# Sinks apart from the table exponential, wide norm statistics between large products, and late windowed output adds on GpSimd, in a hybrid attention and ConvFFN layer

## The chip, the cores and the metric

The kernel runs on one core of a Trainium2 chip. Four compute engines work side by side, each on its own queue of instructions in program order: TensorE (PE in the profile; its weight loads are PEld), VectorE (DVE), ScalarE (ACT) and GpSimd (POOL). SyncE (SP) issues most of the DMAs. Engines meet only at semaphores, so an engine that waits holds back all that is queued behind the waiting instruction. Matmul results lie in PSUM, everything else in SBUF.

The metric is device time in microseconds (us) of one execution, as the median over several. The profile comes from one further execution, whose time is given beside it.

## The reference

One layer over 1024 latent tokens of width 1024, with 256 context tokens that serve as keys and values only. The layer's input is modulated by a conditioning vector. It then goes through two attention branches in parallel, a gated merge, a first norm, a gated ConvFFN and a second norm. Cut to what the change touches:

```python
def _sink_softmax(scores, sink):
    sink = sink.astype(jnp.float32)[:, :, None, None]
    m = jnp.maximum(jnp.max(scores, axis=-1, keepdims=True), sink)
    e = jnp.exp(scores - m)
    return e / (jnp.sum(e, axis=-1, keepdims=True) + jnp.exp(sink - m))

def _layer_norm(x, g, b):
    mu = jnp.mean(xf, axis=-1, keepdims=True)
    var = jnp.mean(jnp.square(xf - mu), axis=-1, keepdims=True)
    return ((xf - mu) * lax.rsqrt(var + LN_EPS) * g + b).astype(x.dtype)

h = x * (1.0 + scale1) + shift1
# branch A: 8 heads on 2 key heads, keys within 128 tokens and the context, sinks
o_a = _windowed_attention(q_a, k_a, v_a, k_a_c, v_a_c, sink)
# branch B: 8 heads on 2 key heads, all keys and the context
o_b = _global_attention(q_b, concat([k_b, k_b_c]), concat([v_b, v_b_c]))
y = (g_a * (o_a @ w_branch_a) + g_b * (o_b @ w_branch_b)) @ w_out
x = _layer_norm(ALPHA * x + gate1 * y, ln1_g, ln1_b)
y = _conv_ffn(x * (1.0 + scale2) + shift2, w_up, conv_w, conv_b, w_down)
x = _layer_norm(ALPHA * x + gate2 * y, ln2_g, ln2_b)
```

## The kernel before

**Arithmetic.** Every large float32 product is made of three fp32r matmuls: an operand is split into a high and a low part, and `mm3` (L89 to L92) adds high x high, high x low and low x high in PSUM. The split itself is `split` (L77 to L87): a copy gives the high part (L82 on ScalarE, L84 on GpSimd), a subtraction the low part (L87 on VectorE or GpSimd). A big matmul has 512 columns.

**Stages, in program order.** First the modulation and the input projections, with the gates in `sgd` on DRAM. Then attention, with the output projection of each branch (`b`) filled in between. Then the merge and `w_out` (`y`) with the first norm, the ConvFFN with its products, and the second norm at the end.

**Attention.** 32 units `Unit(br, i, g)` run one after another: branch 0 (windowed, units 0_0_0 to 0_7_1) and then branch 1 (global, 1_0_0 on). `i` is one of 8 blocks of 128 tokens and `g` one of two key heads, with four query heads each. Where the branch is plain, a unit is written by i and g alone, (6,1) for 0_6_1; so are the tile names in the listings of the change (`up_6_0`). The profile prints tile names without any of these numbers. For each head `lat` makes the scores on TensorE (`s`, L494 and L495), VectorE scales them and takes their maximum (L545, tile `p`), and ScalarE takes the exponential with its sum (L547). In branch 0 each row of probabilities gets one more column, the sink of the head, which GpSimd writes two at a time (L542, from `sinkb`). `norm` (L562) inverts the sums. `rows` puts them as rows into `rb` by way of DRAM.

The steps of unit u's scores are laid between the value steps of the unit before. A value step (`tr_step`) transposes a block of 128 keys for four heads on TensorE (L605, into PSUM tile `ptr`, three buffers) and splits it: ScalarE writes the high part `pth` (L614), VectorE the low part `ptl` (L615). In branch 0, block 3 of the units with `i` from 1 to 6 (in branch 1 two blocks of each unit but the last) goes another way and is called `pooled`: ScalarE copies it into one of two `side` tiles in SBUF (L611), and GpSimd makes both parts (L84 and L87). After a lag of some steps `av_step` multiplies both parts with the values (L626, L627) into the one PSUM tile `av`. After a unit's last block `out_step` copies `av` to a `side` tile (L638 on ScalarE), GpSimd moves its upper half to `up` (L639), two adds join the halves into `ot` (L642; VectorE in branch 0, GpSimd in branch 1 but for the last unit), GpSimd multiplies by `rb` (L645) and splits into the operands `O` (L84, L87). `side` has two tiles in turn, `up` and `ot` one buffer each. The next units' queries are transposed on TensorE (`qtr`), copied by ScalarE (L487, tile `q`), and scaled or split on GpSimd (`qs`).

Between the gates' last sigmoid and attention's first exponential, L871 makes exp(-2^100) = 0 in `zero`, with the load of ScalarE's table of exponentials in front of it. L872 adds this zero to `sinkb` on GpSimd.

**The norms.** `ln_add` sums each finished slice of z and its squares into `zs` and `zq`. `ln_steps` returns the steps of one slice's norm: `stats` (sums over the features by TensorE, one matmul of one column for each 128 tokens and each of `zs` and `zq`, L1186 and L1187, tile `st`, then some small operations), `diags`, `cast` (broadcast of the rows) and eight `apply` steps. Each step carries a distance. A list `pend` holds the steps and a counter `clock`; after each `mm3` of a large product, `tick` adds HALF / 0.8 = 640 for its 512 columns, and a step is issued as soon as the counter reaches its distance, which is then taken off. The order on TensorE is thus fixed when the program is built. The first norm has slices a0 (512 tokens) and smaller ones, the second b0 (512 tokens) and two of 256.

The lines that the change edits stand in `tr_step` (L608), `out_step` (L640), behind `zero` (L872) and in `ln_steps` (L1179 to L1186, L1218):

```python
pooled = n in POOL_LO[self.br] and not last and (self.br or 0 < self.i < NT - 1)
oe = nc.gpsimd if self.br and not last else nc.vector
nc.gpsimd.tensor_tensor(out=sinkb[:, 0:4], in0=sinkb[:, 0:4], in1=zero, op=ALU.add)
for t in range(n):
    ts = slice(s.start + t * P, s.start + (t + 1) * P)
    nc.tensor.matmul(st[:, t:t + 1], zs[:, ts], onec, start=True, stop=True)
    nc.tensor.matmul(st[:, n + t:n + t + 1], zq[:, ts], onec, start=True, stop=True)
```

Of the kernel before, what the change touches and what calls it, by code (L numbers as in the profile page):

```python
# [10 lines left out]
ALU = mybir.AluOpType  # L11
AX = mybir.AxisListType

P = 128
# [4 lines left out]
NT = 8  # L19
# [8 lines left out]
HALF = 512  # L28
FBIG = 3.0e38
POOL_LO = (3,), (2, 6)  # L30
# [39 lines left out]
def layer_kernel(  # L70
# [6 lines left out]
    nc = tc.nc  # L77
# [27 lines left out]
    sinkb = ctile([P, 8], F32, "sinkb")  # L105
# [7 lines left out]
    onec = ctile([P, 1], F32, "onec")  # L113
# [171 lines left out]
    for k in range(KT):  # L285
# [10 lines left out]
        for a in (0, 4):  # L296
            ts = [slice(t * P, (t + 1) * P) for t in range(a, a + 4)]
# [166 lines left out]
    class Unit:  # L464
# [131 lines left out]
        def value_steps(self):  # L596
            nm, kt = self.id, self.kt
            vh = self.br * 2 + self.g
            last = self.id == f"1_{NT - 1}_1"
            parts = {}  # L600

            def tr_step(n):
                tr = pt_tile(f"ptr{nm}_{n}")
                for h in range(4):
                    nc.tensor.transpose(tr[:, h * P:(h + 1) * P], self.pslice(h, n), ident)  # L605
                hi = att.tile([P, 512], R32, tag="pth", name=f"pth{nm}_{n}", bufs=4)
                lo = att.tile([P, 512], R32, tag="ptl", name=f"ptl{nm}_{n}", bufs=4)
                pooled = n in POOL_LO[self.br] and not last and (self.br or 0 < self.i < NT - 1)  # L608
                if pooled:
                    rw = side_tile()  # L610
                    nc.scalar.copy(rw, tr)  # L611
                    split(rw, hi, lo, nc.gpsimd, nc.gpsimd)
                else:
                    nc.scalar.copy(hi, tr)  # L614
                    nc.vector.tensor_tensor(out=lo, in0=tr, in1=hi.bitcast(F32), op=ALU.subtract)  # L615
                parts[n] = hi, lo
                return pooled

            def av_step(n):
                first = self.left == len(kt)  # L620
                self.left -= 1
                if first:
                    self.av = ps2.tile([P, 512], F32, tag="av", name=f"av{nm}")
                hi, lo = parts.pop(n)
                v = VT[kt[n] // 2][:, kt[n] % 2, vh]
                nc.tensor.matmul(self.av, v, hi, start=first, stop=False)  # L626
                nc.tensor.matmul(self.av, v, lo, start=False, stop=self.left == 0)  # L627

            def out_step():
                av = self.av  # L630
                up = att.tile([HD, 512], F32, tag="up", name=f"up{nm}", bufs=1)
                ot = att.tile([P, 2, P], F32, tag="ot", name=f"ot{nm}", bufs=1)
                if last:
                    low = av
                    nc.scalar.copy(up, av[HD:P])
                else:
                    low = side_tile()
                    nc.scalar.copy(low, av)  # L638
                    nc.gpsimd.tensor_scalar(out=up, in0=low[HD:P], scalar1=1.0, scalar2=0.0, op0=ALU.mult, op1=ALU.add)  # L639
                oe = nc.gpsimd if self.br and not last else nc.vector  # L640
                for h in range(2):
                    oe.tensor_tensor(out=ot[h * HD:(h + 1) * HD],  # L642
                                     in0=low[0:HD].rearrange("p (a b q) -> p a b q", b=2, q=P)[:, :, h],
                                     in1=up.rearrange("p (a b q) -> p a b q", b=2, q=P)[:, :, h], op=ALU.add)
                (nc.vector if last else nc.gpsimd).tensor_tensor(out=ot, in0=ot, in1=self.rb, op=ALU.mult)  # L645
                hf = self.i // 4
                qs = slice((self.i % 4) * P, (self.i % 4 + 1) * P)
                split(ot, otile(self.br, hf, 0, self.g)[:, :, qs], otile(self.br, hf, 1, self.g)[:, :, qs],
                      *((nc.scalar, nc.vector) if last else (nc.gpsimd, nc.gpsimd)))

            def step(ns):
                pooled = [tr_step(n) for n in ns]
                for n, pl in zip(ns, pooled):
                    clk[0] += 1
                    avq.append((self, n, clk[0] + LAG[self.br] + (PLAG[self.br] if pl else 0)))
                    av_issue()

            self.left = len(kt)
            self.av_step, self.out_step = av_step, out_step
            g = 1 + self.br  # L660
            steps = [lambda n=n: step(range(n, n + g)) for n in range(0, len(kt), g)]
            steps.insert(3 if self.br else 2 if self.i else len(steps), self.rows)
            return steps
# [155 lines left out]
    for n, (gi, k) in enumerate(order):  # L819
# [8 lines left out]
        if gi == "g":  # L828
            for hf in (0, 1):
                last = gate(k, hf)  # L830
# [8 lines left out]
        nm, src, tiles = groups[gi]  # L839
# [4 lines left out]
        for t in tiles:  # L844
            if t < NT:
                s = slice(t * P, (t + 1) * P)
                a = hT[k][0][:, s], hT[k][1][:, s]
            else:
                s = slice((t - NT) * P, (t - NT + 1) * P)
# [19 lines left out]
    zero = ph1.tile([P, 4], F32, tag="zero", name="zero")  # L869
    nc.vector.tensor_scalar(out=zero, in0=last[:, 0:4], scalar1=-(2.0 ** 100), scalar2=None, op0=ALU.min)  # L870
    nc.scalar.activation(zero, zero, AF.Exp)  # L871
    nc.gpsimd.tensor_tensor(out=sinkb[:, 0:4], in0=sinkb[:, 0:4], in1=zero, op=ALU.add)  # L872
    hTp.release()
    ph1.release()
    ps1.release()
# [100 lines left out]
    for u in range(nu + 1):  # L976
# [8 lines left out]
        if u == 31:  # L985
            first = branch_steps(1, w_b, (0, 1), att, (nc.gpsimd, nc.gpsimd), (0,))
# [15 lines left out]
        while adds:  # L1002
            t, m = adds.pop(0)
# [50 lines left out]
    def sml(name, w=512):  # L1054
        return ps3.tile([P, w], F32, tag="sml", name=name, bufs=2)
# [41 lines left out]
    for f in range(2, KT):  # L1097
# [4 lines left out]
        for hs in halves:  # L1102
            n = HALF * len(hs)
# [36 lines left out]
    def ln_flush():  # L1140
        while sqs:
            sqs.pop(0)()
# [30 lines left out]
    def ln_steps(zs, zq, s, nm, emit, first, gap, gap1, gap2, each, pm=2, order=range(KT)):  # L1173
        w = s.stop - s.start
        n = w // P
        bcs = []
        sv = []

        def stats():  # L1179
            ln_flush()  # L1180
            sv.extend(tiny(f"{a}{nm}") for a in ("mv", "m2", "rs", "mr"))
            mv, m2, rs, mr = sv
            st = sml(f"st{nm}")
            for t in range(n):
                ts = slice(s.start + t * P, s.start + (t + 1) * P)
                nc.tensor.matmul(st[:, t:t + 1], zs[:, ts], onec, start=True, stop=True)  # L1186
                nc.tensor.matmul(st[:, n + t:n + t + 1], zq[:, ts], onec, start=True, stop=True)  # L1187
            nc.vector.tensor_scalar(out=mv[:, 0:2 * n], in0=st[:, 0:2 * n], scalar1=1.0 / D, scalar2=None,
                                    op0=ALU.mult)
            nc.vector.tensor_tensor(out=m2[:, 0:n], in0=mv[:, 0:n], in1=mv[:, 0:n], op=ALU.mult)  # L1190
            nc.vector.scalar_tensor_tensor(out=rs[:, 0:n], in0=mv[:, n:2 * n], scalar=LN_EPS, in1=m2[:, 0:n],
                                           op0=ALU.add, op1=ALU.subtract)
            nc.gpsimd.tensor_tensor(out=rs[:, 0:n], in0=rs[:, 0:n], in1=mhalf[:, 0:n], op=ALU.pow)
            nc.vector.tensor_tensor(out=mr[:, 0:n], in0=mv[:, 0:n], in1=rs[:, 0:n], op=ALU.mult)

        def diags():
            bcs.extend(diag(c[:, 0:n], n, f"{a}{nm}") for a, c in zip("rm", sv[2:]))

        def cast():
            both = sml(f"bc{nm}") if 2 * w <= HALF else None  # L1200
            for i, a in enumerate("rm"):
                ps = sml(f"bc{a}{nm}")[:, 0:w] if both is None else both[:, i * w:(i + 1) * w]
                nc.tensor.matmul(ps, onesf, bcs[i], start=True, stop=True)
                bcs[i] = ps
            mean = post.tile([P, HALF], F32, tag="mrs", name=f"mb{nm}", bufs=2)[:, 0:w]
            nc.scalar.copy(mean, bcs[1])
            bcs.append(mean)

        def apply(f):
            zf = zv(f, s)  # L1210
            nc.vector.tensor_tensor(out=zf, in0=zf, in1=bcs[0], op=ALU.mult)
            if (f + 1) % pm:
                nc.vector.tensor_tensor(out=zf, in0=zf, in1=bcs[1], op=ALU.subtract)
            else:
                nc.gpsimd.tensor_tensor(out=zf, in0=zf, in1=bcs[2], op=ALU.subtract)
            emit(f, s)

        return [(first, stats), (gap, diags), (gap1, cast)] + [(gap2 if n == 0 else each, lambda f=f: apply(f))  # L1218
                                                for n, f in enumerate(order)]

    zs, zq = tm("zs1"), tm("zq1")
# [121 lines left out]
    for f in (4, 6):  # L1343
        for si in (1, 2):
# [3 lines left out]
            elif f == 6:  # L1348
                (_, st), (_, dg), (_, ca), *ap = ln1(si)
                n = len(pend) - 4  # L1350
# [375 lines left out]
    s = LN2_S[-1]  # L1726
# [10 lines left out]
    st = pst(ab[2], "stl")  # L1737
# [57 lines left out]
    sv = [post.tile([P, 2 * nt], F32, tag=f"{n}l", name=f"{n}l") for n in ("mv", "m2", "rs")]  # L1795
# [142 lines left out]
```

## Time and profile before

| | |
|---|---|
| Time, median of 3 runs (lowest to highest) | 1548.82 us (1548.79 to 1549.32) |
| Profiled execution: its time, its span | 1549.4 us, 1547.5 us |
| Granted TensorE clock over the span | 0.996 |
| Windowed attention starts (first exponential) | 335.7 us |
| Passage from windowed to global attention | about 445 to 480 us |
| Statistics of slice a0 of the first norm | 833.3 to 835.5 us |
| Statistics of slice b0 of the second norm | 1475.6 to 1477.3 us |

How the rows of the profile are read. A row of the timeline has the start (us from the span's start), the duration in us, engine, line, operation, what is written and read, shape and type, how many instructions it stands for, and in brackets how long the engine had been idle before it and who ended that wait ("<-ACT p L547" is ScalarE's instruction of line 547). A row of a stretch has its bounds, its length, TensorE's busy time with the number of its instructions, the granted clock as a share of full speed, the busy share of the DMA engines and the GB/s that they moved. Matmuls are pipelined: a row's duration may be longer than the distance to the next start.

### The profile page before, as it was taken

The numbers are of one execution on the slowest core, as the hardware profiler recorded it, in microseconds if no ns is written. First come the engines' busy times: TensorE is split into PE (matmuls) and PEld (weight loads), VectorE is DVE, ScalarE is ACT, GpSimd is POOL, SyncE is SP. The second block draws the span as 40 slices with busy tenths as digits, with TensorE's granted clock in tenths as the row PEclk, the third lists the DMA queues.
The fourth block names the chain that finished last, engine by engine and source line by source line (L and its number), as shares of the span: only waits on it lengthen the run. The fifth ranks groups of instructions, "written<-read, shape, count | busy, mean of one in ns | idle before, by whom it ended". The sixth has DMA issues, their size and how long they took to land.

```text
span 1547.5 us, 22251 instructions
## 1 busy us (share of the span) xinstructions
PE 1528.1 (99%) x7804; PEld 1281.6 (83%) x7804; DVE 1173.3 (76%) x1768; ACT 786.6 (51%) x1271; POOL 751.3 (49%) x738
## 2 busy tenths in 40 slices
PE   9999999999999999999999999999999999999997
PEld 7888888888877888888888998888888888888887
DVE  6677976538888777777774788888888887657884
ACT  5322222458977676667332564444444444435552
POOL 0356522517765666666233345666677674111121
PEclk9999999999999999999999999999999999999998
DMA  9777673322234576563550322333344447996731
GB/s 372 266 240 245 204 252 88 103 75 70 64 85 116 125 167 135 137 150 81 207 177 14 107 88 94 110 112 117 109 106 112 110 109 204 356 266 209 257 103 55
DMA packets 114400, 232.09 MB, mean 150 GB/s; under 512 B 13201, under 2 KB 28049, under 8 KB 114193
## 3 DMA queue, kind: packets, MB, share of 16 engines
q1 hardware_dynamic: 99056, 201.82, 39.2%
q0 software_dynamic: 10400, 20.19, 8.7%
q10 hardware_dynamic: 4832, 8.68, 1.5%
q8 instruction: 61, 1.00, 0.3%
q14 instruction: 51, 0.41, 0.1%
HBM read 179.45 MB, written 65.86 MB: 159 GB/s over the span
## 4 chain that ended last, share of the span: by engine, by line
PE 89%; DVE 3%; issue 3%; ACT 3%; POOL 1%; DMA 1%; SPq 0%; DVEq 0%; ACTq 0%; POOLq 0%
PE ptr L605 6%; PE p L90 4%; PE p L92 4%; PE p L91 4%; PE g L91 3%; PE g L90 3%; PE g L92 3%; PE av L626 3%; PE b L90 3%; PE av L627 3%; PE b L91 3%; PE b L92 3%; PE s L495 2%; PE s L494 2%; PE c L90 2%
## 5 line engine op out<-in xcount | busy, mean ns | idle before, releaser
L547 ACT ACTIVATE p<-p,nm 128x1280 f32<-128x1280 f32 (+2 forms) x128 | 139.1, 1088 | 27.7 <-DVE p L545 27.1
L615 DVE TENSOR_TENSOR ptl<-ptr,pth 128x512 fp32r<-128x512 f32 x194 | 129.3, 685 | 29.7 <-ACT pth L614 27.6
L605 PE MATMUL ptr<-ident,p 128*128 128x128 f32 x944 | 141.0, 276 | 2.6 <-ACT p L547 1.2
L614 ACT CAST pth<-ptr 128x512 fp32r<-128x512 f32 x194 | 110.4, 586 | 44.3 <-PE ptr L605 35.6
L87 DVE TENSOR_TENSOR ld<-rd,hd 128x1024 fp32r<-128x1024 f32 x77 | 94.8, 1249 | 49.9 <-ACT hd L82 47.8
L605 PEld LDWEIGHTS ptr<-ident,p 128*128 128x128 f32 x944 | 108.7, 140 | 28.5 <-ACT q L487 5.4
L82 ACT CAST hd<-rd 128x1024 fp32r<-128x1024 f32 x77 | 79.4, 1050 | 80.3 <-PE p L92 54.0
L87 POOL TENSOR_TENSOR wlg<-wg,whg 128x512 fp32r<-128x512 f32 x32 | 46.6, 1467 | 123.3 <-ACT whg L82 123.3
L626 PE MATMUL av<-pth,VT 128*128 128x512 f32 x236 | 103.8, 440 | 1.3 <-ACT side L638 0.8
L90 PE MATMUL p<-hd 128*128 128x512 f32 x264 | 103.2, 391 | 0.0
L92 PE MATMUL p<-hd,ld 128*128 128x512 f32 x264 | 102.7, 389 | 0.0
L91 PE MATMUL p<-ld,hd 128*128 128x512 f32 x264 | 102.7, 389 | 0.0
L90 PE MATMUL g<-hh,whg 128*128 128x512 f32 x256 | 99.9, 390 | 0.0
L92 PE MATMUL g<-hh,wlg 128*128 128x512 f32 x256 | 99.7, 389 | 0.0
L91 PE MATMUL g<-hl,whg 128*128 128x512 f32 x256 | 99.6, 389 | 0.0
L627 PE MATMUL av<-ptl,VT 128*128 128x512 f32 x236 | 97.4, 413 | 1.5 <-POOL ptl L87 1.4
L545 DVE TENSOR_SCALAR_CACHE_REDUCE p<-s,cvt,nmc 128x1024 f32<-128x1024 f32 x64 | 84.2, 1317 | 10.6 <-PE s L495 10.4
L494 PE MATMUL s<-KL,q 128*128 128x512 f32 (+2 forms) x192 | 75.0, 390 | 0.6 <-DVE p L545 0.6
L495 PE MATMUL s<-KL,q 128*128 128x512 f32 (+2 forms) x192 | 72.0, 375 | 0.0
L82 ACT CAST wS<-s 128x512 fp32r<-128x512 f32 x76 | 45.3, 620 | 50.9 <-POOL s L1237 50.1
L782 ACT ACTIVATE sg<-g,bgc 128x512 f32<-128x512 f32 x32 | 21.9, 686 | 96.2 <-PE g L92 91.5
L82 ACT CAST wA<-ru 128x512 fp32r<-128x512 f32 x57 | 35.5, 623 | 63.2 <-PE d L92 34.4
(438 smaller groups left out, 4878.6 us busy)
## 6 DMA issues: line engine op xcount, KB each, us to landing
wml<-in_wmodT_dram SPq DMA_DIRECT2D x48, 512.0 KB
ru<-in_w_up_dram SPq DMA_DIRECT2D x38, 512.0 KB
rd<-td SPq DMA_DIRECT2D x55, 256.0 KB
rd<-sd SPq DMA_DIRECT2D x44, 256.0 KB
rd<-in_w_dn_dram SPq DMA_DIRECT2D x33, 256.0 KB
wm<-in_wmodT_dram SPq DMA_DIRECT2D x16, 512.0 KB
wg<-in_w_g_dram SPq DMA_DIRECT2D x32, 256.0 KB
sgd<-sg ACTq DMA_DIRECT2D x32, 256.0 KB
```

The source lines that it names most:

```text
L82: nc.scalar.copy(hi, src)
L87: lo_eng.tensor_tensor(out=lo, in0=src, in1=hi.bitcast(F32), op=ALU.subtract)
L90: nc.tensor.matmul(ps, a[0], b[0], start=start, stop=False, skip_group_check=resumed)
L91: nc.tensor.matmul(ps, a[0], b[1], start=False, stop=False, skip_group_check=resumed)
L92: nc.tensor.matmul(ps, a[1], b[0], start=False, stop=stop, skip_group_check=resumed)
L494: nc.tensor.matmul(o, self.q[0][:, hs], ks, start=True, stop=False)
L547: nc.scalar.activation(row, row, AF.Exp, bias=self.nm[:, hs], scale=-1.0, accum_out=self.sm[:, hs])
L605: nc.tensor.transpose(tr[:, h * P:(h + 1) * P], self.pslice(h, n), ident)
L614: nc.scalar.copy(hi, tr)
L615: nc.vector.tensor_tensor(out=lo, in0=tr, in1=hi.bitcast(F32), op=ALU.subtract)
L626: nc.tensor.matmul(self.av, v, hi, start=first, stop=False)
L627: nc.tensor.matmul(self.av, v, lo, start=False, stop=self.left == 0)
```

## The change

Four edits. First, the condition `pooled` for branch 0 counts units instead of blocks and ends with 0_6_0, so that unit 0_6_1 no longer splits its block 3 on GpSimd; it is then split on ScalarE and VectorE like the others. Second, the adds of `out_step` go to GpSimd for the last four units of branch 0 too (0_6_0 to 0_7_1). Third, the add of `zero` to `sinkb` is gone, while `zero` itself, its exponential and the table load stay. Fourth, in slices of 512 tokens the pairs of statistics matmuls become steps of their own, 640 apart in `tick`'s counter; the last pair stays in `stats`. Slices of 256 tokens are as before.

```diff
-                pooled = n in POOL_LO[self.br] and not last and (self.br or 0 < self.i < NT - 1)
+                pooled = n in POOL_LO[self.br] and not last and (self.br or 2 <= 2 * self.i + self.g < 2 * NT - 3)
...
-                oe = nc.gpsimd if self.br and not last else nc.vector
+                oe = nc.gpsimd if (self.br or self.i >= NT - 2) and not last else nc.vector
...
     nc.scalar.activation(zero, zero, AF.Exp)
-    nc.gpsimd.tensor_tensor(out=sinkb[:, 0:4], in0=sinkb[:, 0:4], in1=zero, op=ALU.add)
...
+        def stat_mm(t):
+            if t == 0:
+                ln_flush()
+                sv.append(sml(f"st{nm}"))
+            st = sv[0]
+            ts = slice(s.start + t * P, s.start + (t + 1) * P)
+            nc.tensor.matmul(st[:, t:t + 1], zs[:, ts], onec, start=True, stop=True)
+            nc.tensor.matmul(st[:, n + t:n + t + 1], zq[:, ts], onec, start=True, stop=True)
+
         def stats():
-            ln_flush()
+            for t in range(0 if n < 4 else n - 1, n):
+                stat_mm(t)
+            st = sv.pop()
             sv.extend(tiny(f"{a}{nm}") for a in ("mv", "m2", "rs", "mr"))
             mv, m2, rs, mr = sv
-            st = sml(f"st{nm}")
-            for t in range(n):
-                ts = slice(s.start + t * P, s.start + (t + 1) * P)
-                nc.tensor.matmul(st[:, t:t + 1], zs[:, ts], onec, start=True, stop=True)
-                nc.tensor.matmul(st[:, n + t:n + t + 1], zq[:, ts], onec, start=True, stop=True)
...
-        return [(first, stats), (gap, diags), (gap1, cast)] + [(gap2 if n == 0 else each, lambda f=f: apply(f))
+        lead = [(HALF / 0.8 if t else first, lambda t=t: stat_mm(t)) for t in range(n - 1 if n >= 4 else 0)]
+        return lead + [(HALF / 0.8 if lead else first, stats), (gap, diags), (gap1, cast)] + [(gap2 if n == 0 else each, lambda f=f: apply(f))
                                                 for n, f in enumerate(order)]
```

**GpSimd at the passage.** Before, GpSimd's queue holds there the output of unit 6_0 (`up`, `ot`, `O`) with the split of block 3 of unit 6_1 (`pth_6_1_3`, `ptl_6_1_3`) in between, and then the query split of the third global unit, 1_1_0 (`qs_1_0`):

```order
L639 TENSOR_SCALAR up_6_0_4788<-side 64x512
L84 TENSOR_SCALAR pth_6_1_3_4816<-side 128x512
L645 TENSOR_TENSOR ot_6_0_4789<-ot_6_0_4789,rb_6_0_4635 128x256
L87 TENSOR_TENSOR ptl_6_1_3_4817<-side,pth_6_1_3_4816 128x512
L84 TENSOR_SCALAR O_4287<-ot_6_0_4789 128x2x128
L87 TENSOR_TENSOR O_4288<-ot_6_0_4789,O_4287 128x2x128
L84 TENSOR_SCALAR qs_1_0_5048<-Q_0_544 128x4x64
```

And with the change, GpSimd at the same place:

```order
L639 TENSOR_SCALAR up_6_0_4787<-side 64x512
L642 TENSOR_TENSOR ot_6_0_4788<-side,up_6_0_4787 64x256 x2
L645 TENSOR_TENSOR ot_6_0_4788<-ot_6_0_4788,rb_6_0_4634 128x256
L84 TENSOR_SCALAR O_4286<-ot_6_0_4788 128x2x128
L87 TENSOR_TENSOR O_4287<-ot_6_0_4788,O_4286 128x2x128
L84 TENSOR_SCALAR qs_1_0_5046<-Q_0_544 128x4x64
```

The two splits of 6_1 are gone, and the two adds of 6_0 have come in ahead of L645.

**VectorE at the passage.** Before, VectorE has the adds of 6_0 (`ot_6_0`) between the sums of unit 7_0 (`sm_7_0`) and the low parts of 6_1 and 7_0:

```order
L562 RECIPROCAL sm_7_0_4710<-sm_7_0_4710 128x4
L642 TENSOR_TENSOR ot_6_0_4789<-side,up_6_0_4788 64x256 x2
L615 TENSOR_TENSOR ptl_6_1_4_4830<-ptr_6_1_4_4824,pth_6_1_4_4829 128x512
L615 TENSOR_TENSOR ptl_7_0_0_4843<-ptr_7_0_0_4837,pth_7_0_0_4842 128x512
L545 TENSOR_SCALAR p_7_1_0_4854,nm_7_1_4835<-s_7_1_0_4848,negsink 128x512
```

With the change VectorE has at this place:

```order
L562 RECIPROCAL sm_7_0_4709<-sm_7_0_4709 128x4
L615 TENSOR_TENSOR ptl_6_1_3_4816<-ptr_6_1_3_4810,pth_6_1_3_4815 128x512
L615 TENSOR_TENSOR ptl_6_1_4_4828<-ptr_6_1_4_4822,pth_6_1_4_4827 128x512
L615 TENSOR_TENSOR ptl_7_0_0_4841<-ptr_7_0_0_4835,pth_7_0_0_4840 128x512
L545 TENSOR_SCALAR p_7_1_0_4852,nm_7_1_4833<-s_7_1_0_4846,negsink 128x512
```

The two adds are gone, and the low part of block 3 of 6_1 has come in their place.

**TensorE at slice a0 of the first norm.** Before, the four pairs (`zs`, `zq` into `sta`) stand in a row between two groups of the `w_out` product `y`:

```order
L92 MATMUL y_512_512_9112<-mh_8702,lwo_8710 128x512
L1186 MATMUL sta_9136<-onec,zs_8811 128x1
L1187 MATMUL sta_9136<-onec,zq_8812 128x1
L1186 MATMUL sta_9136<-onec,zs_8811 128x1
L1187 MATMUL sta_9136<-onec,zq_8812 128x1
L1186 MATMUL sta_9136<-onec,zs_8811 128x1
L1187 MATMUL sta_9136<-onec,zq_8812 128x1
L1186 MATMUL sta_9136<-onec,zs_8811 128x1
L1187 MATMUL sta_9136<-onec,zq_8812 128x1
L90 MATMUL y_512_512_9112<-mh_8747,hwo_8709 128x512
```

With the change the first two pairs stand there as follows, and the other two likewise behind the next groups:

```order
L92 MATMUL y_512_512_9110<-mh_8700,lwo_8708 128x512
L1184 MATMUL sta_9130<-onec,zs_8809 128x1
L1185 MATMUL sta_9130<-onec,zq_8810 128x1
L90 MATMUL y_512_512_9110<-mh_8745,hwo_8707 128x512
L91 MATMUL y_512_512_9110<-ml_8746,hwo_8707 128x512
L92 MATMUL y_512_512_9110<-mh_8745,lwo_8708 128x512
L1184 MATMUL sta_9130<-onec,zs_8809 128x1
L1185 MATMUL sta_9130<-onec,zq_8810 128x1
L90 MATMUL y_512_512_9110<-mh_8780,hwo_8707 128x512
```

Between two pairs there are now three big matmuls, and with them the last pair comes three groups later than before.

## Prediction

> **What bounds the kernel now.** I read the page first (busy shares, then the chain of work that ended last), then TensorE's busy time by stretches, then the timeline around each stretch in which TensorE is not full.
>
> ```profile
> span 1547.5 us, 22251 instructions
> PE 1528.1 (99%) x7804; PEld 1281.6 (83%) x7804; DVE 1173.3 (76%) x1768; ACT 786.6 (51%) x1271; POOL 751.3 (49%) x738
> ...
> PE 89%; DVE 3%; issue 3%; ACT 3%; POOL 1%; DMA 1%; SPq 0%; DVEq 0%; ACTq 0%; POOLq 0%
> ```
>
> TensorE (PE) is busy for 99% of the span and carries 89% of the chain. No other engine comes near, so an edit here can gain only where TensorE waits or runs slowly: 1547.5 - 1528.1 = 19.4 us of idle in all, much of it at the two ends of the program, plus any stretch at a reduced clock. Three stretches lie where the change edits (columns of the rows below: stretch, length, PE busy with its instructions, granted clock, DMA share, GB/s).
>
> ```profile
> 330.00:340.00 10.00, 8.99 (x68) 1.00 0.32 94
> 445.00:480.00 35.00, 32.03 (x195) 1.00 0.27 76
> 830.00:840.00 10.00, 9.83 (x45) 0.83 0.01 2
> ```
>
> The first is the start of windowed attention, 1.0 us idle. The second is the passage from windowed to global attention, 3.0 us idle. In the third TensorE is busy, but its granted clock is 0.83: 1.7 us of work is lost there without being idle. These 5.7 us are, roughly, all that the change can reach.
>
> **Part 1: the sinks no longer wait for the exponential.** The removed line 872 added exp(-2^100) = 0 to the sinks on GpSimd (POOL). It computed nothing, but put GpSimd behind ScalarE's (ACT) exponential of `zero`.
>
> ```profile
> 333.63 1.28 ACT L871 ACT_TABLE_LOAD   x1 [0.39 <-ACT sg L782]
> ...
> 334.38 0.08 DVE L545 DVE_READ_ACCUMULATOR p<-s,negsink 128x1 f32 x1
> ...
> 334.92 0.21 ACT L871 ACTIVATE zero<-zero 128x4 f32<-128x4 f32 x1
> ...
> 335.20 0.20 POOL L872 TENSOR_TENSOR sinkb<-sinkb,zero 128x4 f32<-128x4 f32 x1 [23.89 <-ACT zero L871]
> 335.49 0.65 POOL L542 TENSOR_SCALAR p<-sinkb 128x2 f32<-128x2 f32 x4
> 335.72 0.72 ACT L547 ACTIVATE p<-p,nm 128x513 f32<-128x513 f32 x1 [0.59 <-POOL p L542]
> 336.59 0.33 PE L605 MATMUL ptr<-ident,p 128*128 128x128 f32 x1 [1.01 <-ACT p L547]
> ```
>
> The chain reads downward: table load, `zero` done at 334.92 + 0.21 = 335.13, the sinks, the sink column of the first probability tile (L542), the first real exponential at 335.72, and TensorE's first transpose of it at 336.59 after 1.01 us of idle. The scores that this exponential needs were finished by VectorE at 334.46, and GpSimd had stood idle for 23.89 us, so without line 872 the column is written while the table still loads. The table load and `zero` stay where they are on ScalarE. The exponential then starts at 335.13 instead of 335.72: **0.57 us** earlier, allowing 0.02 us for issue. What is late next is that same exponential: TensorE still idles about 0.45 us. ScalarE's new order puts the second exponential ahead of the q copy, which delays that copy by 0.71 - 0.57 = 0.14 us; its reader is a later unit. Bounds: 0 if another wait follows at once, 1.01 if the whole idle goes. I take 0.57.
>
> **Part 2: the last windowed units.** Two edits act together in the 3.0 us. Key block 3 of unit (6,1) is no longer split into its two parts on GpSimd but, as usual, on ScalarE and VectorE (DVE). And the two adds that join the output halves move from VectorE to GpSimd for units (6,0) to (7,1): 4 units, 8 adds.
>
> ```profile
> 449.07 1.19 DVE L642 TENSOR_TENSOR ot<-side,up 64x256 f32<-64x256 f32 x2 [1.07 <-POOL up L639]
> ...
> 450.35 0.74 POOL L645 TENSOR_TENSOR ot<-ot,rb 128x256 f32<-128x256 f32 x1 [0.35 <-DVE ot L642]
> ...
> 451.04 1.27 POOL L87 TENSOR_TENSOR ptl<-side,pth 128x512 fp32r<-128x512 f32 x1
> ...
> 452.37 0.50 PE L627 MATMUL av<-ptl,VT 128*128 128x512 f32 x1 [1.02 <-POOL ptl L87]
> ...
> 458.41 0.85 DVE L642 TENSOR_TENSOR ot<-side,up 64x256 f32<-64x256 f32 x2 [1.09 <-POOL up L639]
> ...
> 459.29 0.69 DVE L615 TENSOR_TENSOR ptl<-ptr,pth 128x512 fp32r<-128x512 f32 x1
> ...
> 460.04 0.66 PE L605 MATMUL ptr<-ident,p 128*128 128x128 f32 x4 [0.45 <-DVE ptl L615]
> ...
> 462.55 0.50 PE L626 MATMUL av<-pth,VT 128*128 128x512 f32 x1 [0.56 <-ACT side L638]
> ...
> 474.23 1.56 DVE L642 TENSOR_TENSOR ot<-side,up 64x256 f32<-64x256 f32 x2
> 475.82 1.34 DVE L545 TENSOR_SCALAR_CACHE_REDUCE p<-s,cvt,nmc 128x1024 f32<-128x1024 f32 x1
> ...
> 477.23 0.50 PE L494 MATMUL s<-KL,q 128*128 128x512 f32 x1 [0.56 <-DVE p L545]
> ```
>
> Three of the four waits go through what is moved. (a) At 452.37 TensorE waited 1.02 us for GpSimd's low part, which sat behind the output chain of (6,0), itself waiting for VectorE's adds. The split no longer runs there; its VectorE half, one more L615 of 0.69 us, falls where VectorE had 1.07 us of idle. (b) At 460.04 it waited 0.45 us for a VectorE subtraction that stood behind two adds of 0.85 us. (c) At 477.23 it waited 0.56 us for a scaling that stood behind two adds of 1.56 us. The fourth, 0.56 us at 462.55, is the round trip through ScalarE to empty the single output bank. Nothing moved stands in it, and I count it only in the upper bound. So the sum is 1.02 + 0.45 + 0.56 = 2.03 us. The idle figures understate each stall, because a 512-column row is drawn 0.39 us long while such matmuls start 0.23 us apart (last part), 0.16 us per wait or 0.48 in all: 2.5 at most from these three, 2.5 + 0.56 + 0.16 = 3.2 with the fourth, and 0 if other waits take their place. I take **2.2 us**, near the sum, since TensorE's order is reshuffled and may lose a little.
>
> What moves to GpSimd is dearer there, and its queue is in order:
>
> ```profile
> 456.45 0.40 POOL L84 TENSOR_SCALAR qs<-Q 128x256 fp32r<-128x256 f32 x1 [2.94 <-PE qtr L484]
> ...
> 480.23 0.62 POOL L84 TENSOR_SCALAR pth<-side 128x512 fp32r<-128x512 f32 x1 [2.31 <-ACT side L611]
> ...
> 491.86 1.53 POOL L642 TENSOR_TENSOR ot<-side,up 64x256 f32<-64x256 f32 x2
> ```
>
> Two adds cost 1.53 us on GpSimd (the same adds as global attention runs them), against 0.85 to 1.56 on VectorE. Behind them wait L645, the output splits, and the next unit's query split, which for (1,1) is now queued after the whole chain of (7,0). The idle of 2.94 and 2.31 us in front of two such starts hides 1.53. If that cover were gone, the price would be 1.53 us per unit; it is a rival below. GpSimd also loses the split of (6,1), and its removed 1.27 us subtraction alone almost pays for one pair.
>
> **Part 3: the statistics of the wide slice.** Each norm sums 512 tokens with eight one-column products in four pairs (zs, zq). Now a pair stands between groups of three big matmuls, so the last three pairs come 1, 2 and 3 groups later.
>
> ```profile
> 832.64 0.39 PE L90 MATMUL y<-mh,hwo 128*128 128x512 f32 x1
> ...
> 833.09 0.39 PE L92 MATMUL y<-mh,lwo 128*128 128x512 f32 x1
> ...
> 833.93 0.38 PE L1187 MATMUL sta<-onec,zq 128*128 128x1 f32 x2 [0.17 <-DVE zq L1154]
> ...
> 835.52 0.67 PE L90 MATMUL y<-mh,hwo 128*128 128x512 f32 x1
> ...
> 839.25 0.39 PE L90 MATMUL y<-mh,hwo 128*128 128x512 f32 x1
> ```
>
> ```profile
> 835.50:836.00 0.50, 0.50 (x4) 0.63 0.00 0
> ...
> 839.00:839.50 0.50, 0.50 (x4) 0.96 0.00 0
> ```
>
> Before the burst, big matmuls start 0.225 us apart (832.64 to 833.09 holds two starts), 0.227 over longer stretches. After it, nine of them take from 835.52 to 839.25, 3.73 us where 9 x 0.227 = 2.04 would do: **1.7 us** lost. The granted clock falls inside 835.5 to 836 and is back just after 839.0. Reading 0.63 and 0.96 as mixtures of full and half clock puts the edges at 835.63 and 839.04. The burst from 833.32 to 835.52, 2.2 us of almost no columns, ends just where the clock halves, and it is the only halving between the two ends of the program. Spread out, no stretch of 3.4 us holds more than about 0.83 + 2 x 0.45 us of pairs and their waits, so I expect the clock to stay full. Bounds: 1.7 gained, or 0 if it halves all the same.
>
> [...]
>
> Do the pairs themselves cost more when spread? The second norm's burst shows entry and exit:
>
> ```profile
> 1475.55 0.28 PE L1186 MATMUL stb<-onec,zs 128*128 128x1 f32 x2
> ...
> 1477.25 0.49 PE L90 MATMUL p<-hd 128*128 128x512 f32 x1
> 1477.57 0.40 PE L91 MATMUL p<-ld,hd 128*128 128x512 f32 x1
> ```
>
> Eight products take 1.70 us. The first big matmul behind them takes 0.32 instead of 0.23, so each extra exit costs 0.09; three exits more in each of two norms make at most 0.54 us. Each extra entry saves about as much, since its weights load behind a big matmul. I take 0, with +0.5 in the range. In this second norm the clock never fell, so there is nothing to win there.
>
> Everything behind the statistics (rows of the norm, its broadcast, the slice's operands) comes three groups, 9 x 0.227 = 2.0 us, later:
>
> ```profile
> 863.25 2.31 DVE L1237 TENSOR_TENSOR B<-z,B 128x512 fp32r<-128x512 f32 x2
> ...
> 880.59 0.40 PE L90 MATMUL u<-B,hwu 128*128 128x512 f32 x1
> ```
>
> VectorE's last operand of the slice is done at 865.56 and first used at 880.59. These 15 us cover the 2.0.
>
> **Sum.** 0.57 + 2.2 + 1.7 = 4.5 us. The profiled execution itself took 1549.4 us (its span of 1547.5 and 1.9 around it): 1544.9. The median of the timed runs, 1548.82, lies 0.58 below it, so the forecast for the median is **1544.3 us**.
>
> **Rivals.** *The half clock stays, or was not in the timed runs.* For it: only one profiled execution shows it, and the second norm's like burst did not cause it. Against it: the burst ends where it begins, and the three timed runs agree within 0.53 us, less than the 1.7 that its coming and going would make. Then 2.8 us remain: 1546.0.
>
> *The passage gives its gain back.* ScalarE's copy of the single output bank (462.55) or its exponentials take the place of the removed waits, because every unit funnels through them. Then 0.57 + 1.7 = 2.3: 1546.5. Against it: VectorE sheds 0.85 to 1.56 us in front of each late step.
>
> *Both, or the edits do nothing that TensorE feels:* only the 0.57 is left, 1548.2.
>
> *GpSimd becomes the bound (slower).* It decides where GpSimd's idle ahead of a piece that TensorE or ScalarE needs is under 1.53 us: ScalarE's copies into the two `side` tiles then wait for GpSimd, and the exponentials queue behind them. With all four units exposed: 4 x 1.53 = 6.1 lost instead of 2.2 won, 1548.8 - 2.3 + 6.1 = 1552.6. The 2.94 and 2.31 us of idle speak against it.
>
> **How the numbers follow.** Forecast 0.54, half clock 0.20, passage 0.15, both 0.05, GpSimd 0.06. The forecast's own range is 1543.1 to 1545.4 (passage 1.6 to 3.2, start 0.3 to 0.8). The range to hold 8 in 10 reaches over the second and third cases with their spread, 1542.7 to 1547.5; the last two cases and thin tails stay outside. About 0.2%, 3.1 us, is what a measurement can tell from no change, so faster means below 1545.7: nearly all of the forecast, a third of the second case and a little of the third, 0.60. Slower is the GpSimd case, 0.06. The rest, 0.34, is within.
>
> **What would show it.** Start: L547's first row about 0.6 us after the table load instead of 0.81, and TensorE's wait there near 0.45. Passage: no wait for GpSimd's low part near 451, no L642 on VectorE after the adds of (5,1), under 1.5 us of idle in the 35 us. Norm: granted clock 1.00 throughout 830 to 850 and big matmuls 0.23 us apart between the pairs. I am wrong if a half-clock stretch stands anywhere between the ends, or if new waits for `side` or GpSimd's `ot` appear.

## The result, and the profile after

The changed kernel took 1545.23 us, median of 11 runs (1544.32 to 1546.25), beside 1548.84 us before (11 runs, 1547.63 to 1550.29). The ratio is 0.9975 with a 95% interval of 0.9966 to 0.9984: 3.6 us faster. The forecast was 1544.3 in a range of 1542.7 to 1547.5. The profiled execution of the changed kernel took 1544.32 us, 5.1 below that of before (1549.4). The forecast sum for the profiles was 4.5. So two questions are open: did the terms come out where they were expected, and why do the profiles differ by more than the medians do?

From the page of the changed kernel, the span, the busy shares and the chain of work that ended last:

```profile
span 1542.5 us, 22261 instructions
PE 1525.4 (99%) x7804; PEld 1279.8 (83%) x7804; DVE 1173.3 (76%) x1761; ACT 787.1 (51%) x1271; POOL 754.2 (49%) x743
...
PE 92%; DVE 3%; ACT 2%; issue 1%; POOL 1%; DMA 0%; SPq 0%; DVEq 0%; ACTq 0%; POOLq 0%
```

The idle of TensorE fell from 19.4 to 17.1 us, and its busy time fell by 2.7 although it has the same 7804 instructions: mostly, those that ran at half clock are short again. The three stretches that the prediction looked at, moved along with the program (stretch, length, busy with instructions, granted clock, DMA share, GB/s):

```profile
329.00:339.00 10.00, 9.68 (x69) 1.00 0.26 87
444.00:477.00 33.00, 32.22 (x202) 1.00 0.28 82
826.00:836.00 10.00, 9.83 (x51) 1.00 0.01 2
```

The start has 0.3 us of idle instead of 1.0, the passage 0.8 instead of 3.0, and the norm a granted clock of 1.00 instead of 0.83. The timeline of the start (start, duration, engine, line, operation; in brackets the idle before and who ended it):

```profile
333.53 1.28 ACT L871 ACT_TABLE_LOAD   x1 [0.39 <-ACT sg L782]
...
334.82 0.20 ACT L871 ACTIVATE zero<-zero 128x4 f32<-128x4 f32 x1
...
334.94 0.71 ACT L547 ACTIVATE p<-p,nm 128x513 f32<-128x513 f32 x1
...
335.79 0.33 PE L605 MATMUL ptr<-ident,p 128*128 128x128 f32 x1 [0.32 <-ACT p L547]
```

The first real exponential now follows `zero` at once, and the sink column (L542) was already written at 332.58, before the table load. The timeline of the passage:

```profile
447.48 0.50 PE L626 MATMUL av<-pth,VT 128*128 128x512 f32 x1 [0.24 <-ACT side L638]
...
448.29 1.52 POOL L642 TENSOR_TENSOR ot<-side,up 64x256 f32<-64x256 f32 x2
448.44 1.29 DVE L615 TENSOR_TENSOR ptl<-ptr,pth 128x512 fp32r<-128x512 f32 x2 [1.26 <-ACT pth L614]
...
459.32 0.40 PE L627 MATMUL av<-ptl,VT 128*128 128x512 f32 x1
459.64 0.66 PE L605 MATMUL ptr<-ident,p 128*128 128x128 f32 x4
...
461.07 0.39 PE L626 MATMUL av<-pth,VT 128*128 128x512 f32 x1
...
469.21 0.66 PE L605 MATMUL ptr<-ident,p 128*128 128x128 f32 x4 [0.54 <-ACT side L611]
```

All four waits quoted before (1.02, 0.45, 0.56 and 0.56 us) are gone, and one of 0.54 has come, for ScalarE's copy of a pooled block of a global unit. The one for the output bank (462.55) went because TensorE's order is another there: between the last product into the bank (459.32) and the first of the next unit (461.07) now stand four transposes and four score products, and ScalarE's copy (0.59 us from 459.75) runs under them. Before, only one small transpose (L566) stood between the two. The timeline of the statistics:

```profile
829.65 0.38 PE L1184 MATMUL sta<-onec,zs 128*128 128x1 f32 x2
830.20 0.38 PE L1185 MATMUL sta<-onec,zq 128*128 128x1 f32 x2 [0.17 <-DVE zq L1153]
830.44 0.47 PE L90 MATMUL y<-mh,hwo 128*128 128x512 f32 x1
...
831.22 0.28 PE L1184 MATMUL sta<-onec,zs 128*128 128x1 f32 x2
831.36 0.36 PE L1185 MATMUL sta<-onec,zq 128*128 128x1 f32 x2
831.58 0.47 PE L90 MATMUL y<-mh,hwo 128*128 128x512 f32 x1
```

The pairs stand one by one between big matmuls, and the big ones start 0.23 us apart.

### The profile page after: what moved, and what is told of

The parts are those of the page before. It is cut to its first block, busy times and chain, and to the rows that moved or that the text cites. A ratio compares the mean times of both kernels' runs of the same rounds, so it can differ in the third digit from the quotient of the medians.

```text
span 1542.5 us, 22261 instructions
## 1 busy us (share of the span) xinstructions
PE 1525.4 (99%) x7804; PEld 1279.8 (83%) x7804; DVE 1173.3 (76%) x1761; ACT 787.1 (51%) x1271; POOL 754.2 (49%) x743
## 4 chain that ended last, share of the span: by engine, by line
PE 92%; DVE 3%; ACT 2%; issue 1%; POOL 1%; DMA 0%; SPq 0%; DVEq 0%; ACTq 0%; POOLq 0%
PE ptr L605 6%; PE p L90 4%; PE p L92 4%; PE p L91 4%; PE g L90 4%; PE g L91 4%; PE g L92 4%; PE av L626 3%; PE av L627 3%; PE b L90 3%; PE b L92 3%; PE b L91 3%; PE s L495 3%; PE s L494 3%; PE c L90 2%; PE c L91 2%
## 5 line engine op out<-in xcount | busy, mean ns | idle before, releaser
L605 PE MATMUL ptr<-ident,p 128*128 128x128 f32 x944 | 141.4, 276 | 1.9 <-DVE ptl L615 0.6
L605 PEld LDWEIGHTS ptr<-ident,p 128*128 128x128 f32 x944 | 108.8, 140 | 28.6 <-ACT q L487 5.6
L627 PE MATMUL av<-ptl,VT 128*128 128x512 f32 x236 | 97.0, 411 | 0.4 <-POOL ptl L87 0.4
```

## The experiments

Where a part gains is read by comparing the start of one and the same TensorE instruction in two traces. The table gives what each stretch gained (-) or lost (+) against the trace of before, in us. **Start**: from the last gate product to the first transpose (L605). **Passage**: from there to the first `sta` product. **Norm**: on to the first `u` product. **Middle**: on to the first `stb` product. **End**: on to the end of the span. Each kernel has one trace. The last column is the median of its runs beside the median of before on the same chip.

| kernel | start | passage | norm | middle | end | medians |
|---|---|---|---|---|---|---|
| changed kernel | -0.70 | -2.94 | -1.53 | -0.03 | +0.32 | 1545.23, 1548.84 |
| r1, changed kernel again | -0.70 | -2.83 | -1.53 | -0.01 | +0.32 | 1544.60, 1549.08 |
| e1, sinks alone | -0.70 | -0.03 | -1.59 | +0.25 | 0 | 1548.57, 1549.08 |
| e2, passage alone | 0 | -2.79 | +0.04 | +1.15 | 0 | 1546.47, 1549.08 |
| e3, statistics alone | 0 | -0.10 | -1.53 | -0.05 | +0.33 | 1548.02, 1549.08 |
| e4, block 3 of (6,1) alone | 0 | -0.89 | -1.56 | +1.09 | 0 | 1548.00, 1549.10 |
| e5, late adds alone | 0 | -0.41 | -1.57 | -0.02 | 0 | 1548.74, 1549.10 |
| e6, second norm not spread | -0.70 | -2.95 | -1.53 | +1.19 | 0 | 1545.27, 1549.10 |

The norm column is already a surprise: e1, e4 and e5 leave the statistics alone and still gain 1.6 there. The middle column has a cost of 1.1 that comes and goes with no edit near it. Both are taken up below; the 0.25 of e1 in that column stays open.

**r1, the changed kernel once more.**

> The changed kernel once more, with a second trace. If the gains of the first two profiles (0.70 at the start, 2.9 at the passage, 1.5 at the norm, 5.1 in all) are those of every execution, the timed difference is near 5 and the trace shows no half-clock stretch between the ends. If the half clock comes and goes whatever the burst does, a trace of the changed kernel can show one too, and the timed difference stays near 3.6. If the profiled execution of before was only a slow draw, the timed difference is 3.6 without any half clock.

The trace repeats the first one within 0.12 us in every stretch, without a half-clock stretch between the ends. The median of 8 runs was 4.5 below before (ratio 0.9973, 0.9963 to 0.9984). The terms are thus stable, while the timed difference lies between 3.6 and 4.5: something in the single executions varies, in before more than here.

**e1, the sinks alone.**

```diff
-    nc.gpsimd.tensor_tensor(out=sinkb[:, 0:4], in0=sinkb[:, 0:4], in1=zero, op=ALU.add)
```

> Line 872 removed from the kernel before and nothing else. Theory: TensorE's first transpose comes 0.57 to 0.75 us earlier against the last gate matmul, its wait shrinks from 1.01 to about 0.5, and all behind it moves by as much: 0.6 us faster. Rival: the time saved is lost at the next waits near 350 and 360, then the time is unchanged within 0.2.

The trace shows 0.70 at the start, kept through attention. The times can't resolve it: ratio 0.9997, 0.9988 to 1.0006.

**e2, the passage alone** (the two lines L608 and L640 of the diff).

> The two edits of the passage alone (block 3 of unit (6,1) off GpSimd, and the output adds of the last four windowed units on GpSimd). Theory: 2.2 to 3.0 us faster, and the same remaining waits as in the changed kernel, 0.8 near 468 and 0.5 near 447. Rival, the passage gains only because the start comes earlier: under 1.5.

2.79 us in the trace, with the wait near 469 that the changed kernel has too; ratio 0.9983 (0.9974 to 0.9991). Here the half clock did stand at the norm, and the time saved at the passage passed through it unharmed.

**e3, the statistics alone.**

> The spread statistics alone. Theory, the burst of small products brings the half clock: no half-clock stretch near 835, and 1.5 to 1.7 us faster. Rival, the half clock depends on where a fixed grid of windows falls in an execution and not on the burst: timed difference near 0 (within 0.5), and the trace may show a half-clock stretch here or elsewhere.

No half clock in the trace and 1.53 us gained there, but the median fell by only 1.1 (ratio 0.9994, 0.9986 to 1.0003). Neither theory fits as stated. The granted clock of the five traces whose first norm still has its burst shows more. The stretch around the burst, in e2 and then in e1 (columns as before):

```profile
830.00:838.00 8.00, 7.83 (x36) 0.79 0.01 2
```

```profile
830.00:840.00 10.00, 9.83 (x51) 1.00 0.01 2
```

In each trace, full clock begins at some time near 5 us (the table has it for five). In before, 128-column products start 0.21 us apart up to 6.15 us and 0.11 apart from 6.29 on. There the half clock lasts 839.04 - 835.63 = 3.41 us and begins 829.44 us behind the start of full clock. Full clock then holds for 699.73 us, and in the trace of the changed kernel for 1529.17 at a stretch. The four lengths are 1, 243, 205 and 448 times one step of 3.4133 us (829.44 / 243). In e2 the first two are the same, and in e7 (below) the half clock begins 431 such steps behind and lasts two. So a grid of windows can be laid over the program, and it is seen how the edges cut the burst:

| trace | full clock from | edge at the burst | small products from, to | largest part in one window | half clock behind |
|---|---|---|---|---|---|
| before | 6.19 | 835.63 | 833.39 to 835.52 | 2.13 | yes |
| e2 | 4.48 | 833.92 | 830.66 to 832.79 | 2.13 | yes |
| e1 | 4.72 | 834.16 | 832.65 to 834.78 | 1.51 | no |
| e4 | 4.02 | 833.45 | 832.58 to 834.71 | 1.26 | no |
| e5 | 4.91 | 834.34 | 833.07 to 835.20 | 1.27 | no |

(Edge = start of full clock + 243 x 3.4133 in all five.) In these five the burst halved the clock just where it fell whole into a window. The second norm's burst of 1.70 us falls whole into a window of the same grid in before (1473.9 to 1477.3), e1, e5 and e9, and halved nothing there. So the limit, for a window at full clock, seems to lie between 1.70 and 2.13 of 3.41 us. If the grid lies anywhere with equal chance, a burst of 2.13 has more than the limit in one window in (3.41 - 2.13 + 2 x (2.13 - limit)) / 3.41 of the executions: 38 to 63%. By this estimate the gain of 1.53 is met in about half of them.

The times agree. From the lowest to the highest of a session they reach over 2.7 to 3.8 us for the kernels with the first norm's burst (before, e1, e2, e4, e5), and over at most 1.9 for those without it (the changed kernel, r1, e3, e6, e8, e9).

**e7, a direct test: the second norm's burst three times as long.** The kernel of e6, with each statistics product of slice b0 issued three times, 24 in a row instead of 8; the result is the same.

```diff
+            for _ in range(3 if nm == "b0" else 1):
...
```

> As the run before, but each statistics product of the second norm's wide slice is issued three times (24 in a row instead of 8, same result). Theory, a window of 3.41 us that is mostly such small products halves the clock for the next window: 16 more products of about 0.21 us, 3.4 us, and a half-clock stretch of at least 3.41 us right behind the burst in every execution, 1.6 us more (one window) or 3.2 (two): 5.0 to 6.6 slower than the run before. Rival, only a TensorE that has nothing to do loses its clock and the stretch before had another cause: 3.4 slower, no half clock near 1475.

TensorE by stretches, first in e6, then here (same columns as above):

```profile
1476.00:1483.00 7.00, 7.00 (x29) 1.00 0.01 2
```

```profile
1472.00:1476.50 4.50, 4.50 (x42) 0.99 0.59 184
1476.50:1483.00 6.50, 6.50 (x21) 0.50 0.09 34
```

And its timeline:

```profile
1474.80 0.36 PE L1186 MATMUL stb<-onec,zq 128*128 128x1 f32 x2
1475.02 0.36 PE L1185 MATMUL stb<-onec,zs 128*128 128x1 f32 x2
...
1478.60 0.63 PE L91 MATMUL p<-ld,hd 128*128 128x512 f32 x1
1479.03 0.63 PE L92 MATMUL p<-hd,ld 128*128 128x512 f32 x1
```

TensorE is busy without a gap (4.50 of 4.50), and the clock goes to 0.50 all the same, for two windows: half clock from 1476.42 to 1483.25. Big matmuls start 0.43 us apart instead of 0.23. Of the program behind the first `stb` product TensorE needs 6.8 us more than in e6, just above the theory's 6.6, and the median is 7.0 higher (1552.29). The rival, that only a TensorE with nothing to do loses its clock, is out. By the grid of this trace the window ahead of 1476.42 holds nothing but small products. The next one holds only 1.6 us of them, run at half clock, and stays halved behind it, so the limit of 1.70 to 2.13 is not that of a window at half clock.

**e4 and e5, the two edits of the passage apart.**

> The kernel before with block 3 of unit (6,1) taken off GpSimd, and nothing else. Theory: the wait of 1.19 (start to start) at 451 for GpSimd's low part is gone, those near 459 and 476 behind VectorE's adds stay; 0.8 to 1.2 us of the passage's 2.75. Rival, the two edits only work together, because the low part now queues on VectorE behind the adds that the other edit moves: under 0.4, with a new wait for VectorE's low part of block 3.

> The kernel before with the output adds of the last four windowed units on GpSimd, and nothing else. Theory: the waits near 459 and 476 go (0.6 and 0.7 start to start), while the one at 451 stays or grows to 1.2 to 1.9, since GpSimd then has two adds of 0.73 more ahead of the low part of (6,1): 0.4 to 1.5 us faster. Rival, this edit alone makes the whole passage gain: 2.7.

Alone they gain 0.89 and 0.41, together 2.8 to 2.9. Why the adds alone gain so little stands in GpSimd's queue in e5:

```profile
449.26 1.52 POOL L642 TENSOR_TENSOR ot<-side,up 64x256 f32<-64x256 f32 x2
450.87 0.62 POOL L84 TENSOR_SCALAR pth<-side 128x512 fp32r<-128x512 f32 x1
451.45 0.73 POOL L645 TENSOR_TENSOR ot<-ot,rb 128x256 f32<-128x256 f32 x1
...
452.14 1.27 POOL L87 TENSOR_TENSOR ptl<-side,pth 128x512 fp32r<-128x512 f32 x1
...
453.46 0.50 PE L627 MATMUL av<-ptl,VT 128*128 128x512 f32 x1 [1.43 <-POOL ptl L87]
```

The adds of (6,0) stand ahead of both parts of (6,1)'s block 3, and TensorE's wait for the low part grows from 1.02 to 1.43 us. In e4 that wait is gone, but two behind VectorE's adds remain (0.3 and 0.7 us from start to start near 458 and 475), with one of 0.4 near 461 for ScalarE's copy of `rb`. So the first edit clears the queue into which the second one moves its work.

**e8, the adds of all windowed units on GpSimd.** This is the rival of the prediction that ended on the slower side.

```diff
-                oe = nc.gpsimd if (self.br or self.i >= NT - 2) and not last else nc.vector
+                oe = nc.gpsimd if (not last) else nc.vector
```

> The changed kernel with the output adds of all sixteen windowed units on GpSimd, not of the last four only. It tests the rival by which GpSimd becomes the bound. From 370 to 445 GpSimd is busy 55.8 of 75 us, 6.0 of the 8.06 us of a unit; two adds more (1.47) make 7.5 of 8.06. Theory: the idle of 2.0 us per unit still hides them, and the time changes by less than 1 us (VectorE is relieved, but TensorE waits for nothing there). Rival: the in-order queue exposes them, up to 1.47 for each of 12 units, 3 to 18 us slower, with TensorE's new waits on side tiles or on GpSimd's low parts from the third unit on.

1560.88 us, beside 1549.35 before (ratio 1.0077, 1.0063 to 1.0091): 15.7 above the changed kernel. My expectation was wrong and the rival's 3 to 18 us held, though a unit lost more than its 1.47: it takes 9.80 us (one and the same product of L627 at 415.81 and 425.61) instead of 8.05, 1.75 more. GpSimd's queue in one unit:

```profile
427.08 0.74 POOL L645 TENSOR_TENSOR ot<-ot,rb 128x256 f32<-128x256 f32 x1
...
428.42 0.74 POOL L87 TENSOR_TENSOR O<-ot,O 128x256 fp32r<-128x256 f32 x1
...
429.28 0.62 POOL L84 TENSOR_SCALAR pth<-side 128x512 fp32r<-128x512 f32 x1
...
429.95 0.50 PE L626 MATMUL av<-pth,VT 128*128 128x512 f32 x1 [0.81 <-POOL pth L84]
...
431.31 0.50 PE L627 MATMUL av<-ptl,VT 128*128 128x512 f32 x1 [0.42 <-POOL ptl L87]
```

The split of block 3 now stands behind the whole output chain, and the output product waits for both of its parts in every unit. Idle time in GpSimd's total (2.0 us per unit) was no cover, since it lay behind the split and not ahead of it.

**e6, the second norm's statistics in one burst again.** It tests the end of the program, where the three traces with spread statistics so far lose 0.3.

```diff
-            for t in range(0 if n < 4 else n - 1, n):
+            for t in range(n - 1 if nm == "a0" else 0, n):
...
-        lead = [(HALF / 0.8 if t else first, lambda t=t: stat_mm(t)) for t in range(n - 1 if n >= 4 else 0)]
+        lead = [(HALF / 0.8 if t else first, lambda t=t: stat_mm(t)) for t in range(n - 1 if nm == "a0" else 0)]
```

> The changed kernel, but with the statistics of the second norm's wide slice in one burst as before; only the first norm's are spread. Theory: TensorE up to its last matmul as in the changed kernel (no half clock at the first norm, and none at the second, whose burst of 1.7 us is half a window), and the 0.3 us that all three kernels with spread statistics lose between the last matmul and the end (10.10 against 9.80) come back: 0.3 us faster than the changed kernel, fast group of times near 1544.2. Rival, the 0.3 have another source: the end stays at 10.1 and the times are the same.

In the trace the 0.3 us come back. They lie at one place, ScalarE's last instruction, in the timeline of the changed kernel, of e6 and of e8:

```profile
1534.42 0.72 ACT L1819 ACTIVATE ot<-ot,rsl 128x512 f32<-128x512 f32 x1 [3.04 <-POOL rsl L1810]
```

```profile
1535.41 0.72 ACT L1819 ACTIVATE ot<-ot,rsl 128x512 f32<-128x512 f32 x1 [2.76 <-POOL rsl L1810]
```

```profile
1550.60 0.72 ACT L1819 ACTIVATE ot<-ot,rsl 128x512 f32<-128x512 f32 x1 [2.76 <-POOL rsl L1810]
```

It waits 0.28 us longer in the changed kernel. But e8 spreads the second norm's statistics too and doesn't wait longer, so the spread alone is not the cause, and my theory falls. Nothing in the traces shows another; it stays open. The median (1545.27) is that of the changed kernel, so spreading the second norm neither pays nor clearly costs, and no version run here beats the changed kernel beyond doubt.

**e9, e6 without `zero`** (its tile, L870 and L871 removed).

> The run with only the first norm's statistics spread, and without zero and its exponential: the table load then belongs to the first real exponential. Theory: that exponential needs nothing but the table, starts right after the load instead of behind zero, and all behind comes 0.2 us earlier than in that run (TensorE's wait at the start near 0.3 instead of 0.5); the fast group of times near 1544.1. Rival: the table load is no longer issued while the scores are made but waits with its exponential, then the start is up to 1 us later.

The rival was right: 1545.96 us (ratio to before 0.9977, 0.9968 to 0.9986), 0.7 above e6. ScalarE's timeline:

```profile
334.36 1.28 ACT L547 ACT_TABLE_LOAD   x1 [1.24 <-DVE p L545]
335.66 0.73 ACT L547 ACTIVATE p<-p,nm 128x513 f32<-128x513 f32 x1
```

The table load now belongs to the real exponential and waits with it for the scores. The exponential starts at 335.66, where that of the changed kernel started at 334.94. The loss grows behind it: in the columns of the table this trace has +0.10 at the start and -1.84 at the passage, 1.9 us less than e6 gained there. The medians differ by less; they are of two sessions and also hold the race told next, whose cost e6's trace has and this one lacks. So `zero`, which computes nothing, earns its place by pulling the table load ahead; the line that took it through GpSimd did not.

**The cost in the middle.** It goes with a race of two instructions. VectorE's and GpSimd's timelines in the trace of before, then in e2 with TensorE's wait:

```profile
947.44 2.40 POOL L87 TENSOR_TENSOR wS<-s,wS 128x512 fp32r<-128x512 f32 x1 [2.44 <-ACT wS L82]
947.47 1.22 DVE L1409 TENSOR_TENSOR c<-c,c 128x1024 f32<-128x1024 f32 x1
```

```profile
944.74 1.28 POOL L87 TENSOR_TENSOR wS<-s,wS 128x512 fp32r<-128x512 f32 x1 [2.43 <-ACT wS L82]
944.78 2.33 DVE L1409 TENSOR_TENSOR c<-c,c 128x1024 f32<-128x1024 f32 x1
...
954.33 0.47 PE L90 MATMUL c<-T13h,wS 128*128 128x512 f32 x1 [1.75 <-DVE c L1400]
```

Both engines start within 0.04 us of each other on operands in SBUF, and one of them takes about 1.1 us longer. Where it is VectorE, TensorE waits 1.75 instead of 0.63 us for the product behind. It was VectorE in the traces of e2, e4, e6 and e7, and GpSimd in the other eight. No edit comes near it. GpSimd starts first in all twelve, by 28 to 34 ns where VectorE is slowed and by 22 to 28 where GpSimd is; whether such a small lead decides it, twelve traces do not show.

## Why the prediction was right, and where it was off

**The start** was given 0.57 and brought 0.70. The mechanism was as told; the exponential even starts 0.08 us before the end that is drawn for `zero`, where 0.02 behind it was allowed. The sign named for it, an exponential "about 0.6 us after the table load", did not follow from that sum, which gives 0.24 behind the load's end; it is 0.13.

**The passage** was given 2.2 and brought 2.8 to 2.9, inside its bounds of 0 to 3.2. The three waits named did go. The term was mis-sized at the fourth wait, ScalarE's copy of the output bank: "Nothing moved stands in it, and I count it only in the upper bound." It went as well, since TensorE's order there is another, where the prediction had only allowed that the reshuffled order "may lose a little". One new wait of 0.54 took a part back. That the gain needs both edits was not seen; e5 shows that the adds alone lengthen the first wait.

**The norm** was given 1.7 and brought 1.53 where the half clock had stood. The burst without a half clock (e1, e4, e5) saved 1.56 to 1.59, so the spread pairs cost under 0.1, near the 0 that was taken for them. The step that failed is the one against the first rival: "the three timed runs agree within 0.53 us, less than the 1.7 that its coming and going would make." Three runs were too few. In 30 runs of before on one chip, 13 lie at or below 1548.30 and 8 at or above 1550.07, and times as wide apart are found only with a burst. So the half-clock rival was partly right: the profiled execution had a half clock that, by the estimate above, about half of the executions lack. The edges measured here fit a step of 3.41 us that begins at another time in each trace (4.02 to 6.19 us in the table). Idle time is not what it took: in e7 a TensorE that is busy throughout, by the profile (4.50 of 4.50 us), with one-column products goes to a clock of 0.50.

**The end** was to stay as it was. It is 0.3 longer in three of the four traces with spread statistics, without a cause that the runs show.

**The median.** Start 0.70, passage 2.9 and end -0.3 make 3.3. The means over the two sessions were 1549.03 (41 runs before) and 1545.08 (19 runs after), 3.95 apart. The remaining 0.65 is a little under half of 1.53 and fits the estimate from the windows. The fit is loose, since the race of 1.1 us enters both means with shares that are not known. The two profiled executions differ by 5.1 because that of before was one with the half clock. The forecast of 4.5 had counted the norm in full and the passage short.

**The rivals.** GpSimd did not become the bound, but e8 shows that it would with the adds of earlier units, and for the reason given: the in-order queue, not its busy share.

## What to carry to other kernels

Before work is moved to an engine with idle time, look at what stands behind it in that engine's queue and who waits for it: the same two adds gain where the pooled split is gone (2.79 us in e2, 0.89 without them in e4), and cost 1.75 us a unit where it stands behind them (e8). A stretch at half clock in one profile may be missing in other executions (two of five traces had it here), so count it by the share of executions that have it. Here runs of one-column matmuls of up to 1.7 us cost no clock. When an instruction that computes nothing is removed, ask what it was pulling ahead: of the two that dealt with `zero`, one cost 0.7 us and the other saved at least as much.

## What the runs showed of the hardware

A TensorE that the profile shows busy, with 0.17 us of idle in before and none in e7, dropped to half clock (0.50) behind a 3.41 us window that one-column products filled for the most part: 2.13 us was enough in two traces, 1.70 was not in four, and 24 in a row cost two windows.

Of a VectorE and a GpSimd instruction that start within 0.04 us of each other, one or the other took about 1.1 us longer: VectorE's took 1.22 us in before and 2.33 in e2, GpSimd's 2.40 and 1.28. It was VectorE's in four traces and GpSimd's in eight, with no edit near. Which of the two it was went with 1.1 us of this kernel's time in these traces.
